# Gates, branches and mixer output: high and low input side by side on one load of the high weights, in blocks of 256 features

## The chip, the cores and the metric

The kernel runs on one core of one Trainium2 chip. Times are device microseconds of that core; several runs of a kernel are given as their median. The engines are TensorE (PE, with its weight loads shown as PEld), VectorE (DVE), ScalarE (ACT), GpSimd (POOL) and SyncE (SP), which here issues nearly all DMA transfers.

## The reference

One decoder layer over 256 tokens of 2048 features, in float32. The part that the change touches is the gated merge of the token mixer; the rest (a matrix-memory LSTM, a delta-rule recurrence, cross-attention into 256 memory tokens, a gated feed-forward layer with a short convolution) stays as it is.

```python
h = rms_norm(x, mix_pre_norm)
proj = h @ w_in                                  # 2048 -> 10536 columns
mlstm_p, rwkv_p, gate_p = split_cols(proj, ...)  # gate_p: 4096 columns
# ha: 256 x 1024, output of the mLSTM;  hb: 256 x 1024, output of RWKV-7
g_a, g_b = split_cols(gate_p, (D_MODEL, D_MODEL))
merged = sigmoid(g_a) * (ha @ w_branch_a) + sigmoid(g_b) * (hb @ w_branch_b)
y = merged @ w_out                               # 2048 -> 2048
x = x + rms_norm(y, mix_post_norm)
h = rms_norm(x, xattn_pre_norm);  m = rms_norm(mem, mem_norm)
x = x + rms_norm(cross_attention(h, m, ...), xattn_post_norm)
x = x + rms_norm(conv_glu_ffn(rms_norm(x, ffn_pre_norm), ...), ffn_post_norm)
```

## The kernel before

**Products in three matmuls.** Every float32 operand is split into a high part, rounded to the matmul's input type, and a low part, the rest. A product is then the sum of three: high weights with high input, high weights with low input, low weights with high input. An "fm" block gives features on partitions and the 256 tokens along the free axis; a "tm" block gives tokens on partitions and 512 features along the free axis. `block` (line 365) only notes what is to be done; `run` (line 435) goes through the list and issues everything.

**Narrow and wide fm blocks.** A narrow fm block has 512 output features: each 128 x 128 piece of weights (a step) takes three matmuls of 256 columns, which add up in one half of a PSUM bank; two features groups share a bank, a block has two banks. A wide block (line 475) has 256 output features. High and low input lie side by side in one tile, so that one matmul of 512 columns takes both on one load of the high weights: one half of the bank gets high times high, the other high times low. A second matmul of 256 columns adds low weights times high input to the first half. A wide block of two feature groups also has two banks. Who reads the result has to add the two halves. Before the change only the 58 blocks `w_fw` of the feed-forward layer are wide (line 1662), and `fw_evac` (line 1621) does that addition: two copies on ACT from PSUM, two additions on DVE.

**The way of a weight tile.** `Feed` (line 373) brings the weights in tiles of 512 KB (128 partitions x 1024 values): SP loads `raw` (three buffers), ACT rounds it to `wh` (line 402), DVE subtracts to `wl` (line 423; four buffers each). While tile i is multiplied, `run` issues the subtraction for tile i + 3 and the load for tile i + 6. A load waits until the subtraction three tiles earlier has freed its buffer. A 512-feature block has two k per tile, a block of 256 features four.

**Side work and its budget.** Everything but matmuls and weight casts is written as generators, cut in pieces by `yield`, and handed to `Spread` (line 73). `run` calls `half` once at the start of each weight tile and again between its k: a narrow tile of 512 features gives two calls, a wide one of 256 two as well, and a narrow tile of 256 features would give four. Each call adds 790 to a budget of DVE and 820 to one of ACT (estimated nanoseconds, at most 1200 saved up, at most 700 of debt kept), and then runs at most one piece of `bulk` (the evacuations, in their order) or `back`, if both budgets are positive, and those of `chains` whose turn has come, if neither is below -700. `need` issues all that is left of a task at once. At the start of each block `run` needs the evacuation of two blocks before. The engines then work in the order in which things were issued, each waiting for its operands.

**The order of blocks around the change.** After the projections of both mixers (two tm blocks for the output gate of the mLSTM come last, and `mlstm` runs on as part of the second one's evacuation, line 1140) come, for branch a and then branch b, gate blocks (2048 inputs, weights in `w_in`) ahead of branch blocks (1024 inputs): gate 0, gate 1, branch 0, gate 2, branch 1, gate 3, branch 2, branch 3 (line 1432). `gate_evac` (line 1232) multiplies by the row of inverse norms and applies the sigmoid; `br_evac` (line 1242) multiplies the branch by its gate, in branch b adds branch a, and splits the sum into `mgh` and `mgl`, the inputs of the mixer output. The recurrence (`rwkv`, a chain) runs beside them and ends in `hb_split`, which branch b needs (line 1399). Before branch b's last block `mem_prep` starts (line 1407): a chain with a piece every third call that loads the memory tokens in four transfers on SP, splits them and sums their squares; its sums over partitions are matmuls on PE (`st`, `stb`).

Then four mixer blocks (line 1455). `mo_xs` needs the last branch's evacuation when it comes to k = 12. Before the second mixer block `load_x` (line 1443) loads x again, 2 MB in two transfers on SP's queue. `y_evac` (line 1262) sums squares of the result and writes it, times a gain, to `z`; after the last block `column_of_sums` (line 344) folds the squares on DVE and sums them over partitions on PE. From that, `Residual` (line 1288) forms the new x and the input of the cross-attention's queries; meanwhile PE has the block `w_xk` to do, which needs only the memory tokens, and then `w_xq`, which needs the residual.

Of the kernel before, what the change touches and what calls it, by code (L numbers as in the profile page):

```python
# [15 lines left out]
P = 128  # L16
D = 2048
S = 256
# [134 lines left out]
def _layer(ctx, tc, nc, d, dbg):  # L153
# [119 lines left out]

    def bc(ap, n):
        return ap.unsqueeze(1).broadcast_to((ap.shape[0], n, ap.shape[1]))
# [97 lines left out]
    class Feed:  # L373
# [766 lines left out]
    def mlstm():  # L1140
# [38 lines left out]
        ha = [U(f"ha{i}", dt=F32R) for i in range(2)]  # L1179
        M["ha"] = ha  # L1180
        for k2 in range(4):
# [5 lines left out]
            for j in range(2):  # L1187
                k = k2 * 2 + j
                xsplit_gain(ha[0][:, k], ha[1][:, k], q[:, j], pcol("hn", k))
            yield  # L1190

    def hb_split():
# [6 lines left out]
        hb = [U(f"hb{i}", dt=F32R) for i in range(2)]  # L1199
        M["hb"] = hb  # L1200
# [8 lines left out]
        for p2 in range(4):  # L1209
# [18 lines left out]
            xsplit(hb[0][:, s2], hb[1][:, s2], M["bv"][:, s2])  # L1228
# [3 lines left out]
    def gate_evac(i, cb):  # L1232
        def gen(ps):
            sg = [T2("sg") for _ in range(2)]
            M["sg", i, cb] = sg
            for g in range(2):
                times(sg[g], ps[g], st0.rb)
                act.activation(sg[g], sg[g], AF.Sigmoid)
                yield
        return gen  # L1240

    def br_evac(i, cb):
        def gen(ps):
# [15 lines left out]
        return gen  # L1259


    def y_evac(b, st, key, gname):

        def gen(ps):
            if b == 0:
                M[key] = [U("z0"), U("z1")]
            z = M[key][b // 2]
# [5 lines left out]
            for g in range(2):  # L1273
                if not late:
                    st.add(ps[g])
                for j in range(2):
                    m = (b % 2) * 4 + g * 2 + j
                    act.activation(z[:, m], ps[g][:, j], AF.Copy, scale=pcol(gname, b * 4 + g * 2 + j))
                if g or not late:
                    yield  # L1280
            if b == 3 and not late:
# [591 lines left out]
```

## Time and profile before

| | us |
|---|---|
| median of 3 runs (1826.32 to 1827.95) | 1826.34 |
| the profiled execution | 1827.7 |
| its span | 1825.9 |
| PE busy, of the span | 1806.5 (99%) |
| DVE busy | 1349.3 (74%) |
| ACT busy | 1071.2 (59%) |
| mean granted TensorE clock | 0.997 |

The span runs from the first to the last instruction of the profiled execution; the time of that execution includes what lies around it. Rows of instruction views give start, duration (both in us from the span's start), engine, line, operation, output and inputs, shape and number; in brackets how long the engine was idle before, and for whom. Rows of windows give the stretch, its length, the busy time of PE, PEld, DVE, ACT and POOL (instructions in brackets), the granted clock, the DMA share and GB/s. Rows of the chain give start, length and what. Matmuls overlap in the pipe, so the duration in their rows is longer than the distance from one to the next. Line 66 is that of a helper through which all side work goes; there the tile names tell what it is: `sg` gates and branch sums, `mgh`/`mgl` the mixer's input, `mx`, `mem`, `stm` of `mem_prep`, `sty` and `z` of `y_evac`, `us`, `ul` of `fw_evac`.

### The profile page before, as it was taken

How to read it: one execution, taken by the hardware profiler on the slowest of the kernel's cores; microseconds unless marked ns; L12 is line 12 of the kernel's file. 1: busy time of each engine (PE TensorE's matmuls, PEld its weight loads, DVE VectorE, ACT ScalarE, POOL GpSimd, SP SyncE). 2: the span in 40 equal slices, each digit the busy share in tenths (PEclk: the TensorE clock that was granted, in tenths of full speed). 3: DMA queues.
4: the chain of work that ended last, by engine and by line, in shares of the span. 5: the costliest groups of instructions: out<-in, count | busy, mean ns of one | idle time of the engine just before them, and what ended most of it. 6: DMA issues, size and time to landing. Idle time of an engine off the chain costs nothing.

```text
span 1825.9 us, 32950 instructions
## 1 busy us (share of the span) xinstructions
PE 1806.5 (99%) x13182; PEld 1687.7 (92%) x13182; DVE 1349.3 (74%) x1954; ACT 1071.2 (59%) x1616; POOL 30.6 (2%) x53
## 2 busy tenths in 40 slices
PE   9999999999999999999999999999999999999998
PEld 8999988999999999899899999999999988888887
DVE  6879985666766766868887887877877876666665
ACT  6577355554544565666676767665656655555553
POOL 0100000000100000000000000000000000000000
PEclk9999999999999999999999999999999999999999
DMA  7655554354656675546566666666666666666664
GB/s 260 203 169 189 166 187 151 113 179 147 190 178 203 220 254 175 184 143 202 180 210 202 202 199 203 202 196 208 201 199 205 199 199 212 222 201 203 201 204 160
DMA packets 97899, 352.50 MB, mean 193 GB/s; under 512 B 11057, under 2 KB 11313, under 8 KB 97361
## 3 DMA queue, kind: packets, MB, share of 16 engines
q1 hardware_dynamic: 96496, 348.07, 59.8%
q8 instruction: 103, 1.69, 0.4%
q0 software_dynamic: 384, 1.18, 0.3%
q10 hardware_dynamic: 864, 1.15, 0.2%
q14 instruction: 52, 0.42, 0.1%
HBM read 347.73 MB, written 2.10 MB: 192 GB/s over the span
## 4 chain that ended last, share of the span: by engine, by line
PE 92%; DVE 4%; DMA 2%; issue 1%; ACT 1%; POOL 0%; DVEq 0%; POOLq 0%; ACTq 0%
PE fm L189 64%; PE tm L189 23%; DVE wl L423 1%; ACT wh L402 0%; DMA raw<-in_w_in_dram 0%; PE gram L189 0%; DMA raw<-in_w_mo_dram 0%; PE Y L189 0%; DVE ql L66 0%; DMA x<-in_x_dram 0%; PE lv L189 0%; DVE tg L66 0%; PE num L189 0%; DVE z L66 0%; PE X L189 0%
## 5 line engine op out<-in xcount | busy, mean ns | idle before, releaser
L423 DVE TENSOR_TENSOR wl<-raw,wh 128x1024 fp32r<-128x1024 f32 x640 | 780.2, 1222 | 319.5 <-ACT wh L402 316.1
L402 ACT CAST wh<-raw 128x1024 fp32r<-128x1024 f32 x640 | 669.4, 1048 | 372.6 <-PE fm L189 211.3
L189 PE MATMUL fm<-fx,wh 128*128 128x512 f32 (+1 forms) x2240 | 673.1, 364 | 0.6 <-ACT fx L66 0.6
L189 PE MATMUL fm<-fx,wl 128*128 128x256 f32 x2048 | 559.2, 273 | 1.5 <-DVE wl L423 1.3
L189 PEld LDWEIGHTS fm<-fx,wh 128*128 128x128 f32 x2240 | 409.1, 190 | 49.8 <-ACT fx L66 0.8
L189 PEld LDWEIGHTS fm<-fx,wl 128*128 128x128 f32 x2048 | 393.2, 192 | 3.2 <-DVE wl L423 3.2
L189 PE MATMUL fm<-hx,wh 128*128 128x256 f32 x2144 | 367.4, 278 | 1.2 <-ACT wh L413 1.2
L189 PEld LDWEIGHTS fm<-hx,wh 128*128 128x128 f32 x2144 | 327.0, 193 | 3.4 <-ACT hx L66 1.4
L189 PE MATMUL tm<-wh,as 128*128 128x512 f32 x1024 | 304.6, 379 | 0.0
L189 PE MATMUL fm<-hx,wl 128*128 128x256 f32 x1072 | 295.7, 276 | 0.5 <-DVE wl L423 0.4
L189 PEld LDWEIGHTS tm<-wh,as 128*128 128x128 f32 x1024 | 193.5, 189 | 27.5
L189 PEld LDWEIGHTS fm<-hx,wl 128*128 128x128 f32 x1072 | 206.5, 193 | 0.9 <-DVE wl L423 0.6
L189 PE MATMUL tm<-wl,as 128*128 128x512 f32 x512 | 194.0, 379 | 0.0
L189 PEld LDWEIGHTS tm<-wl,as 128*128 128x128 f32 x512 | 96.8, 189 | 13.7
L66 ACT CAST as<-ac 128x256 fp32r<-128x256 f32 x128 | 45.4, 402 | 104.0 <-PE tm L189 104.0
L66 DVE TENSOR_TENSOR as<-ac,as 128x256 fp32r<-128x256 f32 x128 | 48.5, 421 | 53.7 <-ACT as L66 53.7
L66 ACT COPY ul<-fm 128x256 f32<-128x256 f32 x116 | 40.6, 374 | 72.6 <-PE fm L189 72.6
L189 PE MATMUL tm<-wh,hx 128*128 128x512 f32 x256 | 77.2, 383 | 0.0
L189 PE MATMUL fm<-mgh,wl 128*128 128x256 f32 x256 | 70.5, 275 | 0.2 <-DVE wl L423 0.2
L189 PE MATMUL fm<-mgh,wh 128*128 128x256 f32 x256 | 70.6, 276 | 0.0
L189 PE MATMUL fm<-mgl,wh 128*128 128x256 f32 x256 | 70.4, 275 | 0.0
L66 DVE TENSOR_TENSOR us<-fm,ul 128x256 f32<-128x256 f32 x116 | 43.7, 419 | 26.3 <-ACT ul L66 26.3
(355 smaller groups left out, 1979.8 us busy)
## 6 DMA issues: line engine op xcount, KB each, us to landing
raw<-in_w_fw_dram SPq DMA_DIRECT2D x232, 512.0 KB, 4.0
raw<-in_w_in_dram SPq DMA_DIRECT2D x160, 512.0 KB, 3.5
raw<-in_w_fd_dram SPq DMA_DIRECT2D x128, 512.0 KB, 3.9
raw<-in_w_br_dram SPq DMA_DIRECT2D x32, 512.0 KB, 3.9
raw<-in_w_mo_dram SPq DMA_DIRECT2D x32, 512.0 KB, 3.8
raw<-in_w_fu_dram SPq DMA_DIRECT2D x24, 512.0 KB, 3.7
raw<-in_w_xk_dram SPq DMA_DIRECT2D x8, 512.0 KB, 3.5
raw<-in_w_xq_dram SPq DMA_DIRECT2D x8, 512.0 KB, 3.4
```

Source lines behind the costliest of these rows:

```text
L66: return f(out, *a, **k)
L189: pe.matmul(out, lhsT, rhs, start=start, stop=stop, skip_group_check=True)
L402: nc.scalar.copy(wh, r)
L423: nc.vector.tensor_sub(wl, r, self.st[self.nl][0])
```

## The change

The gate blocks, the branch blocks and the mixer blocks become blocks of 256 features: 16 gate blocks (their weights now in an array `w_g` of their own), 16 branch blocks, 8 mixer blocks. All are wide but the last four of branch b, which stay narrow, with three matmuls a step. The number of weight tiles and their size stay. `AHEAD` goes from 2 to 4, so that the same number of gate features is ahead of the branches; `mem_prep` now starts before the seventh block of branch b, `load_x` runs before the third mixer block.

`ha`, `hb` and `mg` are laid out so that high and low part of a k lie in one tile. The copies and additions of `fw_evac` move into a function `whole` with a tag of its own (two buffers), in which the sum is written over the copy; the gate, branch and mixer evacuations call it and then go on from SBUF. They handle one pair of features groups where they handled two. In branch b the evacuation has a second `yield`, after the product. The tiles for `wh` and `wl` lose 128 values of padding per partition, and so does `as` in the down projection, which also loses its offset of 112 values.

```diff
+    def whole(ps):
+
+        w = mp.tile([P, 2, S], F32, tag="lo", bufs=2, name="lo")
+        for i in range(2):
+            act.copy(w[:, i], ps[i][:, 1])
+        for i in range(2):
+            dve.tensor_add(w[:, i], ps[i][:, 0], w[:, i])
+        return w
...
-            w = wp.tile([P, 1024 + 128], F32R, tag=name, bufs=4, name=name)
+            w = wp.tile([P, 1024], F32R, tag=name, bufs=4, name=name)
...
-        ha = [U(f"ha{i}", dt=F32R) for i in range(2)]
-        M["ha"] = ha
+        M["ha"] = [U(f"ha{i}", [P, 2, 4, S], F32R) for i in range(2)]
...
     def gate_evac(i, cb):
         def gen(ps):
-            sg = [T2("sg") for _ in range(2)]
-            M["sg", i, cb] = sg
-            for g in range(2):
-                times(sg[g], ps[g], st0.rb)
-                act.activation(sg[g], sg[g], AF.Sigmoid)
-                yield
+            sg = M["sg", i, cb] = T2("sg")
+            times(sg, whole(ps), st0.rb)
+            act.activation(sg, sg, AF.Sigmoid)
+            yield
...
-                M["mg"] = [big("mgh", dt=F32R), big("mgl", dt=F32R)]
-            for g in range(2):
-                s2 = slice(cb * 4 + g * 2, cb * 4 + g * 2 + 2)
-                pa = M["pa"][cb // 2][:, (cb % 2) * 4 + g * 2:(cb % 2) * 4 + g * 2 + 2]
-                if i == 0:
-                    dve.tensor_mul(pa, ps[g], sg[g])
-                else:
-                    dve.tensor_mul(sg[g], ps[g], sg[g])
-                    dve.tensor_add(sg[g], sg[g], pa)
-                    xsplit(M["mg"][0][:, s2], M["mg"][1][:, s2], sg[g])
-                yield
+                M["mg"] = [big(f"mg{j}", [P, 2, 8, S], F32R) for j in range(2)]
+            s2 = slice(cb % 4 * 2, cb % 4 * 2 + 2)
+            pa = M["pa"][cb // 4][:, s2]
+            w = whole(ps) if len(ps) == 2 else ps[0]
+            if i == 0:
+                dve.tensor_mul(pa, w, sg)
+            else:
+                dve.tensor_mul(sg, w, sg)
+                yield
+                dve.tensor_add(sg, sg, pa)
+                mg = M["mg"][cb // 4]
+                xsplit(mg[:, 0, s2], mg[:, 1, s2], sg)
+            yield
...
-    def y_evac(b, st, key, gname):
+    def y_evac(b, st, key, gname, wide=False):
...
+            if wide:
+                ps = [whole(ps)]
...
     def gated(i, cb, before):
-        xs = lambda k: (M[("ha", "hb")[i]][0][:, k], M[("ha", "hb")[i]][1][:, k])
-        return block("fm", W("w_br", i * 4 + cb), xs, br_evac(i, cb), before=before)
-
-    AHEAD = 2
+        v = lambda k: M[("ha", "hb")[i]][k // 4][:, :, k % 4]
+        return block("fm", W("w_br", i * 8 + cb), lambda k: (v(k)[:, 0], v(k)[:, 1]), br_evac(i, cb), before=before,
+                     cols=256, wide=None if i and cb > 3 else v)
+
+    AHEAD = 4
     for i in range(2):
-        for cb in range(4 + AHEAD):
+        for cb in range(8 + AHEAD):
             if cb >= AHEAD:
                 before = None
                 if cb == AHEAD:
                     before = need_hb if i else lambda: side.need(o1["task"])
+                elif cb == 6 + AHEAD and i:
+                    before = start_mem
                 br = gated(i, cb - AHEAD, before)
-            if cb < 4:
-                block("fm", W("w_in", 12 + i * 4 + cb), xs0, gate_evac(i, cb))
-    br["before"] = start_mem
+            if cb < 8:
+                block("fm", W("w_g", i * 8 + cb), xs0, gate_evac(i, cb), cols=256, wide=lambda k: hx[:, :, k])
...
-    for b in range(4):
-        block("fm", W("w_mo", b), mo_xs, y_evac(b, sty, "z1", "postg"),
-              before=load_x if b == 1 else None)
+        return mgp(k)[:, 0], mgp(k)[:, 1]
+
+    for b in range(8):
+        block("fm", W("w_mo", b), mo_xs, y_evac(b, sty, "z1", "postg", True), before=load_x if b == 2 else None,
+              cols=256, wide=mgp)
...
-            us, lo = T2("us"), T2("ul")
-            for i in range(2):
-                act.copy(lo[:, i], ps[i][:, 1])
-            for i in range(2):
-                dve.tensor_add(us[:, i], ps[i][:, 0], lo[:, i])
+            us = whole(ps)
...
-            a = mp.tile([P, 1024 + 128], F32R, tag=f"au{n % 2}", bufs=1, name="as")[:, 112:112 + 1024]
+            a = mp.tile([P, 1024], F32R, tag=f"au{n % 2}", bufs=1, name="as")
```

More of the change, by code (lines that the diff above doesn't have):

```diff
@@ L1188, in mlstm @@
                 k = k2 * 2 + j
[L1189 removed]
+                ha = M["ha"][k // 4][:, :, k % 4]
+                xsplit_gain(ha[:, 0], ha[:, 1], q[:, j], pcol("hn", k))
             yield
@@ L1272, in gen @@
                 st.column()
[L1273 removed]
+            for g, v in enumerate(ps):
                 if not late:
[L1275 removed]
+                    st.add(v)
                 for j in range(2):
[L1277 to L1279 removed]
+                    m = b * len(ps) * 2 + g * 2 + j
+                    act.activation(z[m // 8][:, m % 8], v[:, j], AF.Copy, scale=pcol(gname, m))
+                if g == len(ps) - 1 or not late:
                     yield
[L1281 removed]
+            if b == (7 if wide else 3) and not late:
                 yield from st.column_of_sums()
```

17 lines of the change are left out of this document (9 added, 8 removed).

## The prediction

> **What bounds the kernel now.** I read the share of each engine, then the chain that ended last in order of time, then the stretches from the gates to the cross-attention by windows, and last the instructions of VectorE (DVE), ScalarE (ACT) and the DMA queue around the end of the branches, where the windows show the least room.
>
> ```profile
> PE 1806.5 (99%) x13182; PEld 1687.7 (92%) x13182; DVE 1349.3 (74%) x1954; ACT 1071.2 (59%) x1616; POOL 30.6 (2%) x53
> 512.45 128.65 PE fm L189 x1152
> 899.05 586.93 PE fm L189 x3583
> 1485.97 327.65 PE tm L189 x1518
> ```
>
> TensorE (PE) bounds it. The three rows of the chain are unbroken runs of matmuls, so a division gives what one costs: three of 256 columns are 3 x 128.65/1152 = 335.0 ns (second branch and first mixer block); a 512 and a 256 together 2 x 586.93/3583 = 327.6 ns (the wide blocks of the feed-forward layer); a 512 alone 327.65/1518 = 215.8 ns (down projection). 335.0/3 = 111.7, and 215.8 + 111.7 = 327.5: the rows agree, and two 256s on one load cost 2 x 111.7 - 215.8 = 7.6 ns more apart than as one 512.
>
> **The matmuls.** One step (a 128 x 128 piece of weights) goes from three matmuls to two, from 335.0 to 327.6 ns: 7.4 ns. Steps changed: gates 8 blocks x 16 k x 4 = 512; branches 8 x 8 x 4 = 256 less 4 x 8 x 2 = 64 left narrow = 192; mixer 4 x 16 x 4 = 256; together 960. 960 x 7.4 = **7.1 us** less. The bytes and the count of weight casts stay.
>
> The page "TensorE: Matmul & The Clock Gate" of the Trainium skill (section Back-to-back issue gap) gives a lone warm matmul N/2.4 + 2.5 ns, with the warning that a stream with weight loads behaves otherwise; by it two 256s cost only 2.5 ns more than one 512, and the gain would be 960 x 2.5 = 2.4 us. The 215.8 ns agrees with it; the 111.7 ns (109.2 by the formula) does not, and the sum goes by the rows.
>
> **The new evacuation.** `whole` adds two copies on ACT and two additions on DVE to each of 16 + 12 + 8 = 36 blocks (gates, branches, mixer). The feed-forward blocks do the same work:
>
> ```profile
> 1202.72 0.70 ACT L66 COPY ul<-fm 128x256 f32<-128x256 f32 x2 [1.34 <-PE fm L189]
> 1203.13 0.76 DVE L66 TENSOR_TENSOR us<-fm,ul 128x256 f32<-128x256 f32 x2 [0.49 <-ACT ul L66]
> 340.00:512.00 172.00, 172.00 (x1988) 169.06 (x1987) 117.00 (x170) 90.57 (x139) 8.88 (x8) 1.00 0.51 167
> 512.00:616.70 104.70, 104.70 (x940) 104.70 (x939) 65.86 (x67) 49.02 (x53) 0.00 (x0) 1.00 0.61 193
> 1000.00:1400.00 400.00, 400.00 (x2444) 367.78 (x2443) 318.22 (x463) 256.52 (x391) 0.00 (x0) 1.00 0.65 201
> ```
>
> 36 x 0.76 = 27 us of DVE and 36 x 0.70 = 25 us of ACT. Averaged over these windows (columns: length, busy PE, weight loads, DVE, ACT, POOL) that is hidden: DVE goes from 68% to some 77% in the first (20 of the blocks), from 63% to 69% in the second (8), and at 318/400 = 80% PE still runs without a gap in the third. If this cover is gone, a block costs up to 0.70 + 0.76 = 1.5 us. The new tag, the removed padding and the moved `as` tile change addresses, not counts: nothing, under the same cover (DVE could slow by a quarter there before it is full). The recurrence's last work, `hb`, has room too:
>
> ```profile
> L66 DVE TENSOR_TENSOR hb<-vT,hb x4: 692/742/743, 499.0 to 515.3; 128x512 fp32r<-128x512 f32 x4
> L189 PEld LDWEIGHTS fm<-hb,wh x256: 192/192/192, 530.9 to 616.5; 128*128 128x128 f32 x128
> ```
>
> It ends 15 us before its reader; nothing is taken for it.
>
> **Where the average hides a place: the last two branch blocks.** `half` hands out the side work. A narrow block of 256 features has four k per weight tile and so four calls of `half` in 2.68 us, where before there were two. `mem_prep` (a piece every third call) starts before branch block 6 at the same point of the matmul stream, but now 16 calls instead of 8 pass until the mixer, with the branch evacuations in the same stretch. Prices:
>
> ```profile
> 605.30:616.70 11.40, 11.40 (x105) 11.40 (x104) 9.20 (x11) 5.48 (x6) 0.00 (x0) 1.00 0.58 192
> 613.34 3.50 DVE L423 TENSOR_TENSOR wl<-raw,wh 128x1024 fp32r<-128x1024 f32 x3 [0.21 <-ACT wh L402]
> 616.75 0.68 DVE L66 TENSOR_TENSOR sg<-fm,sg 128x512 f32<-128x512 f32 x1
> 617.47 0.69 DVE L66 TENSOR_TENSOR sg<-sg,pa 128x512 f32<-128x512 f32 x1
> 619.02 0.76 DVE L66 TENSOR_TENSOR mgl<-sg,mgh 128x512 fp32r<-128x512 f32 x1 [0.86 <-ACT mgh L66]
> 625.64 2.36 DVE L423 TENSOR_TENSOR wl<-raw,wh 128x1024 fp32r<-128x1024 f32 x2 [0.72 <-ACT wh L402]
> 627.92 0.87 DVE L66 SCALAR_TENSOR_TENSOR mx<-mem,par,mx 128x256 fp32r<-128x256 f32 x2
> 628.71 0.68 DVE L66 TENSOR_TENSOR stm<-stm,sq 128x512 f32<-128x512 f32 x1
> 629.31 1.22 DVE L423 TENSOR_TENSOR wl<-raw,wh 128x1024 fp32r<-128x1024 f32 x1
> ```
>
> A weight subtraction (`wl`) takes DVE 3.50/3 = 1.17; a branch evacuation holds it 619.78 - 616.75 = 3.0, the wait for ACT's cast included; a piece of `mem_prep` 629.31 - 627.92 = 1.4 (the first 0.8, without the sum). The budget lets pieces 2 to 5 run before the mixer: it comes back at 790 per call, twice as often in time. DVE then owes, in the 10.7 us of blocks 6 and 7, 4 x 1.17 + 2 x 3.0 + 0.8 + 3 x 1.4 = 15.7 us: 5.0 too much. Blocks 4 and 5 are even (2 x 1.17 + 3.0 = 5.3 of 5.36 each), and so is the mixer's first block (4 x 1.17 + 3.0 + 2 x 1.4 = 10.5 of 10.5). The four 512 KB loads of `mem_prep` move with it in SP's queue, between the raw tiles; the third waits for pieces 2 and 3, but the raw tile behind it waits for a later `wl` of the same DVE anyway, and the DMA share of 0.58 leaves room: nothing more for them. What is late next is `wl`, made three tiles (8.0 us) ahead; with an evacuation in front of it, it is done some 4.5 us into its tile, a reserve of 3.5. So the first mixer tiles wait 5.0 - 3.5 = 1.5, and as the queue doesn't shrink until block 1, the last evacuation too: the new first mixer block needs feature tile k = 14 after 28 x 0.328 = 9.2 us, where the old one needed it after 56 x 0.335 = 18.8. That adds about 1.2. I take **2.7 us**; bounds 0 (the whole 8.0 holds) and 6 (5.0 of lag, and the last evacuation late by 1). For a wait speaks how near it was already: in the rows above, `wl` for the mixer's fifth tile ended at about 626.8, and that tile began at 616.7 + 4 x 2.68 = 627.4: 0.6 us to spare, at half the rate of pieces.
>
> **The x load**, 64 steps into the mixer in both kernels.
>
> ```profile
> 638.93 0.43 SPq L1414 DMA_DIRECT2D mem<-in_mem_dram  x1
> 641.46 0.90 SPq L1447 DMA_DIRECT2D xr<-in_x_dram  x2
> 654.90 0.38 PE L189 MATMUL fm<-mgh,wl 128*128 128x256 f32 x1 [0.19 <-DVE wl L423]
> 658.90 0.61 PE L189 MATMUL st<-ones,stm 128*128 128x1 f32 x4 [1.28 <-DVE stm L66]
> 638.00:648.80 10.80, 10.80 (x99) 10.80 (x98) 8.20 (x12) 10.77 (x19) 0.00 (x0) 1.00 0.88 346
> 648.80:659.50 10.70, 9.23 (x80) 8.85 (x80) 7.06 (x11) 5.44 (x8) 0.00 (x0) 1.00 0.63 229
> ```
>
> Weights queue behind 2 MB of x, and PE waits 0.19 + 1.28 us, the second time in order behind the sum of `mem_prep`. That sum is taken some 12 calls (16 us) earlier now: it moves off x, into the lag just told, and I leave its 1.28 in the sum. Against it, the tiles behind x come due at 2.62 us instead of 2.68, and each mixer block adds 1.5 us of copies and sums in ACT and DVE. **+0.9**; bounds -1.5 (both waits go) and +3 (ACT is 10.77 of 10.80 busy there, so two evacuations of 1.5 could show in full).
>
> **The mixer's end.** The sum of squares of z comes out one `half` earlier, but the new order on DVE is: two additions, square's sum, `wl`, fold.
>
> ```profile
> 705.48 0.83 ACT L66 ACTIVATE z<-fm,par 128x256 f32<-128x256 f32 x2
> 707.13 0.62 ACT L66 ACTIVATE sq<-fm 128x512 f32<-128x512 f32 x1
> 708.42 0.68 DVE L66 TENSOR_TENSOR sty<-sty,sq 128x512 f32<-128x512 f32 x1
> 709.14 0.42 DVE L66 TENSOR_TENSOR sty<-sty 128x256 f32<-128x256 f32 x1
> 709.48 1.22 DVE L423 TENSOR_TENSOR wl<-raw,wh 128x1024 fp32r<-128x1024 f32 x1
> 709.64 0.58 PE st L189 x4
> 720.00:740.00 20.00, 19.67 (x175) 19.33 (x174) 19.83 (x32) 13.60 (x22) 0.00 (x0) 1.00 0.49 156
> 740.00:760.00 20.00, 18.55 (x131) 17.24 (x132) 16.60 (x21) 13.05 (x17) 0.00 (x0) 1.00 0.66 211
> ```
>
> Before, the fold ran ahead of `wl`, and PE's column sums (`st`) came 709.64 - 705.35 = 4.3 us after the mixer's last matmul. Now: copies and additions 1.2, square 0.6, its sum 0.7; ACT meanwhile z 0.8 and cast 1.0, then `wl` 1.2 and fold 0.4: the sums come at 5.2. PE, in order, stands 2.5 us in front of them. What follows is set by DVE (19.83 of 20 us), in which PE idles 0.33 + 1.45 = 1.8 us anyway, so most of the 2.5 is absorbed; what counts is the residual's start, 5.2 - 4.3 = **+0.9** (bounds 0 and 2.5).
>
> **The mLSTM tail.** `run` forces the evacuation of two blocks ago. The first gate block now has 8 calls of `half`, not 16, for eleven pieces of `mlstm`; three transposes of `ha` are forced at once.
>
> ```profile
> 335.73 0.44 PE haT L1186 x4
> 336.71 0.88 DVE L66 SCALAR_TENSOR_TENSOR so<-num,rh,so 128x256 f32<-128x256 f32 x2
> ```
>
> The last waits for `so`, ready at 337.6, and would be reached near 337.1: **+0.5** (bounds 0 and 2, if ACT and DVE are late with casts behind them).
>
> **Sum** against the profiled execution (1827.7, span 1825.9): -7.1 + 2.7 + 0.9 + 0.9 + 0.5 = -2.1, so 1825.6 there; the median is 1826.34 and becomes **1824.2 us**.
>
> **Rivals.** (1) *The lag is hidden.* The reserve holds and x costs nothing new: -7.1 + 0.5 + 0.5 = -6.1, 1820.2. For: averages of 63% to 68% on DVE, a feed-forward at 80% without a gap. Against: the 0.6 us to spare. (2) *Slower: the ring of raw tiles.* A raw buffer comes free only when `wl` is made, so a late `wl` orders its successor late; behind x (7.6 us to land) cast 1.05 and `wl` 1.17, 9.8 us per three tiles of 7.9, lose 1.9 a turn. If the lag is still over the reserve of 3.5 us when x is ordered, it stays through two turns: 6.0 for the branches' end, 3 + 1.9 x 2 at x, 0.9 + 0.5: -7.1 + 14.2 = +7.1, 1833. For: ACT full in that window. Against: from mixer block 1 on, DVE owes 4 x 1.17 + 0.8 + 0.7 + 2.8 = 9.0 of 10.5 us, so 16 us after the overload the lag should be under it.
>
> ```profile
> L402 ACT CAST wh<-raw 128x1024 fp32r<-128x1024 f32 x640 | 669.4, 1048 | 372.6 <-PE fm L189 211.3
> xr<-in_x_dram SPq DMA_DIRECT2D x2, 1024.0 KB, 7.6
> ```
>
> (3) *The change gives less than it says*: a step saves only a third, 2.5 ns, because the 7.4 belongs to the order of loads in its own stage and not to the count of matmuls; 2.4 less and 5.0 back: 1828.9. Against: both rates are from one execution with PE full. The Trainium skill's formula, cited above, gives a saving of this size.
>
> **Chances.** Forecast 0.56 (own range 1821.5 to 1826.8), rival 1 0.26, rival 2 0.10, rival 3 0.04, something unseen 0.04. Range 1819.0 to 1829.0: rival 1 with all its gain at the low end, the upper bounds of the x load and the mixer's end together at the high one. This kernel's measurement tells about 0.2% (3.7 us) from no change: under 1822.7 lie rival 1 and a fifth of the forecast, 0.37; above 1830.0 rival 2 and half of the unseen, 0.12; the rest 0.51.
>
> **What would show it.** Steps: 512-column matmuls at `hx`, `ha`, `mg` and 327.6 ns a pair in unbroken runs. Lag: PE waits for `wl` and `mg` within 15 us of the mixer's start, none there before. Mixer's end: `st` waiting about 2.5 us for `sty`. Wrong: no wait at the mixer's start (rival 1), or waits that last beyond the x load (rival 2).

## The result, and the profile after

| | before | after |
|---|---|---|
| median of 6 runs, us | 1826.55 (1824.83 to 1827.95) | **1837.72** (1834.39 to 1840.59) |
| the profiled execution | 1827.7 | 1834.39 |
| its span | 1825.9 | 1832.6 |
| PE busy | 1806.5 | 1804.0 |

The ratio is **1.0061 [1.0048, 1.0074]**: slower, where 1824.2 was forecast and 1829.0 was the upper end of the range. The profiled execution of after is the fastest of its six; the other five ran at a mean granted clock of 0.995 to 0.997 where it had 0.998 (0.995 in the three runs of 1837.1, 1840.59 and 1840.01). So the trace accounts for 6.7 us of a loss of 11.2, and the clock, to which this text comes back, goes with the rest.

The chain of after (start, length, what) has the long run of the feed-forward layer again, to the hundredth:

```profile
905.54 586.93 PE fm L189 x3583
```

It began at 899.05 before, and all of the loss lies ahead of it. Where, is read from the rows of single tiles: behind the count come the shortest, median and longest instruction in ns, and the times of the first start and the last. First the kernel before, then after:

```profile
L189 PE MATMUL tm<-wl,hx x128: 378/379/379, 216.2 to 315.0; 128*128 128x512 f32 x128
L189 PE MATMUL fm<-ha,wh x256: 275/275/377, 376.7 to 484.0; 128*128 128x256 f32 x128
L189 PE MATMUL fm<-hb,wh x256: 275/275/275, 531.0 to 616.6; 128*128 128x256 f32 x128
L189 PE MATMUL fm<-mgh,wl x256: 275/275/377, 617.0 to 705.3; 128*128 128x256 f32 x128
```

```profile
L189 PE MATMUL tm<-wl,hx x128: 378/379/379, 214.1 to 312.9; 128*128 128x512 f32 x128
L189 PE MATMUL fm<-ha,wh x128: 382/382/483, 379.0 to 485.5; 128*128 128x512 f32 x128
L189 PE MATMUL fm<-hb,wh x192: 275/275/382, 534.0 to 618.1; 128*128 128x256 f32 x128, 128*128 128x512 f32 x64
L189 PE MATMUL fm<-mg,wl x256: 272/273/378, 618.5 to 707.9; 128*128 128x256 f32 x128
```

The starts give the stages. The steps are those of the prediction, at 7.4 ns each:

| stage, us | before | after | difference | by the steps | lost |
|---|---|---|---|---|---|
| up to the last o-gate matmul (ahead of the changed blocks) | 315.0 | 312.9 | -2.1 | 0 | - |
| to the first branch a matmul (128 steps) | 61.7 | 66.1 | +4.4 | -0.9 | **5.3** |
| to the first branch b matmul (384) | 154.3 | 155.0 | +0.7 | -2.8 | **3.5** |
| to the first mixer matmul with low weights (192) | 86.0 | 84.5 | -1.5 | -1.4 | 0 |
| mixer, from there to its last (256) | 88.3 | 89.4 | +1.1 | -1.9 | **3.0** |
| to the long run of the feed-forward layer | 193.7 | 197.6 | +3.9 | 0 | **3.9** |
| from there on | 926.9 | 927.1 | +0.2 | 0 | 0.2 |

The first row is not the work of the changed blocks: up to the first of these matmuls, in code in which the kernels differ only by the padding of `wh` and `wl`, the traces of this document lie between 214.1 and 217.5 us, and in the one of before the clock was halved for 3.4 us at 31.4 us. Counted from the last o-gate matmul, the change's trace is 8.8 us longer. The removed padding does not slow the work on weight tiles either: a cast takes 1047 ns by the median in both traces, a subtraction 1224 and 1225.

The row to the first mixer matmul is the cleanest: no wait in either kernel, 192 steps changed, 1.5 us less. The steps pay what was forecast; 15.7 us are lost in four places. The waits of PE name them (what waited, for whom, us in total, times, longest). Before, the stretches from 313 to 380, 380 to 536 and 705 to 718 us have no wait in this view, and that of the mixer has two:

```profile
PE st L189 <- DVE stm L66: 1.3, 1, 1.3
PE fm L189 <- DVE wl L423: 0.2, 1, 0.2
```

After, from 313 to 380 (the first three rows), from 380 to 536 (the next four) and from 610 to 725 us:

```profile
PE Tn L189 <- ACT au L66: 1.3, 1, 1.3
PE Tn L189 <- DVE au L66: 1.1, 1, 1.1
PE U L189 <- DVE ha L66: 1.0, 2, 0.7
...
PE fm L189 <- DVE wl L432: 0.7, 1, 0.7
PE X L189 <- ACT m L66: 0.7, 1, 0.7
PE zg L189 <- DVE gwl L66: 0.4, 1, 0.4
PE zg L189 <- DVE gwh L66: 0.4, 1, 0.4
...
PE st L189 <- DVE sty L66: 2.9, 1, 2.9
PE st L189 <- DVE stm L66: 1.2, 1, 1.2
PE fm L189 <- DVE wl L432: 1.2, 2, 0.8
PE fm L189 <- DVE mg L66: 0.8, 1, 0.8
PE stb L189 <- POOL sty_c L236: 0.5, 1, 0.5
```

This view counts a wait from the modelled end of the matmul ahead of it and leaves short ones out, so its rows add up to less than a stage lost: 2.2 us of 3.5 from branch a to branch b.

**The burst behind the mLSTM** is the largest. These are rows of the timeline of after, PE's without its block matmuls, then ACT's, then DVE's:

```profile
335.02 1.47 PE L1194 MATMUL haT<-con,so 128*128 128x128 f32 x12
339.46 0.68 PE L189 MATMUL U<-au,mt 64*64 64x64 f32 x16 [0.74 <-DVE ha L66]
345.56 0.33 PE L189 MATMUL Tn<-au,bg 128*64 128x64 f32 x2 [1.29 <-ACT au L66]
347.01 0.62 PE L189 MATMUL Tn<-au,bg 128*64 128x64 f32 x13 [1.12 <-DVE au L66]
...
343.68 0.63 ACT L66 ACTIVATE sg<-sg 128x512 f32<-128x512 f32 x1 [1.50 <-DVE sg L66]
344.21 1.03 ACT L411 CAST wh<-raw 128x1024 fp32r<-128x1024 f32 x1
345.14 0.63 ACT L66 COPY au<-U 64x256 f32<-64x256 f32 x2
...
342.07 0.75 DVE L66 TENSOR_TENSOR lo<-fm,lo 128x256 f32<-128x256 f32 x2
342.85 0.79 DVE L66 TENSOR_TENSOR sg<-lo,st_b 128x512 f32<-128x512 f32 x1
345.27 1.23 DVE L432 TENSOR_TENSOR wl<-raw,wh 128x1024 fp32r<-128x1024 f32 x1 [1.63 <-ACT wh L411]
346.53 0.77 DVE L66 COPY au<-U 64x256 f32<-64x256 f32 x2
```

Twelve transposes come at once, because the second gate block needs all of `mlstm`; ACT and DVE then hand `ha` to and fro until 342 (`U` waits meanwhile), go on with the first gate block's copies, additions, product and sigmoid, then with a cast and its subtraction, and only then copy `U` to `au`. The recurrence's `Tn` stands in PE's order and waits for that copy. The clock then falls, as windows of 3.4 us show (length, busy PE, PEld, DVE, ACT, POOL, granted clock, DMA share, GB/s):

```profile
344.20:347.60 3.40, 0.98 (x22) 0.78 (x23) 2.27 (x4) 2.52 (x5) 0.00 (x0) 0.99 0.05 13
347.60:351.00 3.40, 3.40 (x62) 3.17 (x60) 1.80 (x3) 0.73 (x2) 0.00 (x0) 0.50 0.83 276
```

**The mixer's end**, the second place, in the timeline of after (DVE, then PE without block matmuls):

```profile
708.99 0.75 DVE L66 TENSOR_TENSOR lo<-fm,lo 128x256 f32<-128x256 f32 x2
710.44 0.69 DVE L66 TENSOR_TENSOR sty<-sty,sq 128x512 f32<-128x512 f32 x1 [0.70 <-ACT sq L66]
712.17 1.22 DVE L432 TENSOR_TENSOR wl<-raw,wh 128x1024 fp32r<-128x1024 f32 x1 [1.04 <-ACT wh L411]
713.31 0.42 DVE L66 TENSOR_TENSOR sty<-sty 128x256 f32<-128x256 f32 x1
...
713.78 0.61 PE L189 MATMUL st<-ones,sty 128*128 128x1 f32 x4 [2.89 <-DVE sty L66]
716.34 0.71 PE L189 MATMUL stb<-con,sty_c 128*128 128x128 f32 x4 [0.50 <-POOL sty_c L236]
```

The order on DVE is the one forecast: additions, square's sum, `wl`, fold. The column sums come 713.78 - 707.95 = 5.8 us after the mixer's last matmul, where 5.2 were forecast and 4.3 was the time before.

### The profile page after: what moved, and what is told of

Read it like the earlier page. It is cut to its first block, busy times and chain, and to the rows that moved or that the text cites. A ratio compares the mean times of both kernels' runs of the same rounds, so it can differ in the third digit from the quotient of the medians.

```text
span 1832.6 us, 31158 instructions
## 1 busy us (share of the span) xinstructions
PE 1804.0 (98%) x12222; PEld 1656.2 (90%) x12222; DVE 1375.9 (75%) x2026; ACT 1090.7 (60%) x1688; POOL 32.5 (2%) x53
## 4 chain that ended last, share of the span: by engine, by line
PE 83%; DVE 8%; ACT 3%; DMA 3%; issue 2%; POOL 0%; DVEq 0%; SPq 0%; ACTq 0%; POOLq 0%
PE fm L189 56%; PE tm L189 23%; DVE wl L432 4%; ACT wh L411 2%; DMA raw<-in_w_mo_dram 1%; DVE lo L66 1%; PE Y L189 0%; DMA raw<-in_w_xv_dram 0%; DMA raw<-in_w_g_dram 0%; PE gram L189 0%; DVE z L66 0%; DVE ql L66 0%; ACT z L66 0%; DVE tg L66 0%; DVE sg L66 0%
## 5 line engine op out<-in xcount | busy, mean ns | idle before, releaser
L411 ACT CAST wh<-raw 128x1024 fp32r<-128x1024 f32 x640 | 667.2, 1047 | 332.3 <-PE fm L189 154.7
L189 PE MATMUL fm<-hx,wh 128*128 128x256 f32 (+1 forms) x1632 | 363.3, 312 | 1.0 <-ACT wh L422 1.0
L189 PEld LDWEIGHTS fm<-hx,wh 128*128 128x128 f32 x1632 | 268.0, 192 | 16.1 <-ACT hx L66 1.3
L66 ACT COPY lo<-fm 128x256 f32<-128x256 f32 x188 | 64.4, 372 | 84.9 <-PE fm L189 84.4
L189 PEld LDWEIGHTS tm<-wl,as 128*128 128x128 f32 x512 | 96.8, 189 | 13.7
L66 DVE TENSOR_TENSOR lo<-fm,lo 128x256 f32<-128x256 f32 x188 | 70.9, 419 | 28.2 <-ACT lo L66 28.1
L189 PE MATMUL fm<-mg,wh 128*128 128x512 f32 x256 | 84.7, 383 | 0.8 <-DVE mg L66 0.8
L189 PE MATMUL fm<-mg,wl 128*128 128x256 f32 x256 | 70.2, 274 | 1.3 <-DVE wl L432 1.2
L66 DVE SCALAR_TENSOR_TENSOR tg<-lo,cv,tg 128x255 f32<-128x255 f32 x116 | 55.8, 481 | 2.1
```

The costliest lines, as they stand in the source:

```text
L66: return f(out, *a, **k)
L189: pe.matmul(out, lhsT, rhs, start=start, stop=stop, skip_group_check=True)
L411: nc.scalar.copy(wh, r)
```

## The experiments

All are compared with runs of the kernel before on the same chip (medians 1825.9 to 1826.2). Medians are of 4 to 11 runs.

| kernel | median, us | ratio to before |
|---|---|---|
| the change | 1837.72 | 1.0061 [1.0048, 1.0074] |
| e1: mLSTM tail apart | 1831.51 | 1.0029 [1.0018, 1.0039] |
| e2: fold ahead of `wl` | 1833.97 | 1.0042 [1.0027, 1.0057] |
| e3: two calls a tile | 1837.34 | 1.0060 [1.0038, 1.0082] |
| e4: e1 + e2 + e3 | 1830.11 | 1.0020 [1.0011, 1.0029] |
| e5: e1 + all evacuations cut | 1842.33 | 1.0090 [1.0076, 1.0103] |
| e6: e1 + memory tokens earlier | 1832.95 | 1.0034 [1.0021, 1.0046] |
| e7: e1 + last mixer block narrow | 1829.96 | 1.0020 [1.0011, 1.0030] |
| e8: e5 + e6 + e7 | 1841.05 | 1.0083 [1.0069, 1.0097] |
| e9: e1 + e3, cut where there is room, mixer narrow | **1818.89** | **0.9962 [0.9949, 0.9976]** |
| e10: the change, mixer narrow | 1829.09 | 1.0018 [1.0009, 1.0027] |
| e11: e9, evacuations uncut | 1822.25 | 0.9977 [0.9968, 0.9986] |
| e12: e9, mixer wide but its last block | 1827.39 | 1.0006 [0.9997, 1.0015] |

### One place at a time

**e1, the mLSTM tail as a task of its own**, needed by the first branch block and no longer by the second gate block:

```diff
             if n == 1:
-                yield from mlstm()
+                tasks["ml"] = side.add(mlstm())
...
-                    before = need_hb if i else lambda: side.need(o1["task"])
+                    before = need_hb if i else lambda: side.need(tasks["ml"])
```

> Edit: the mLSTM tail becomes a task of its own, needed by the first branch block, so that the forced evacuation at the start of the second gate block no longer issues three transposes of ha and their splits at once. Theory A (that burst is the largest loss: the recurrence's matmuls U and Tn stand behind it, 2.6 and 2.8 us of PE waiting at 338 to 347 us, and the granted clock falls to half for 3.4 us after it): these waits and the half-clock stretch go, the granted clock of the runs returns to 0.997 or more, and the time falls 5 to 9 us below the changed kernel, to 1829 to 1833. Rival B (the added copies and sums of 36 blocks load DVE and ACT everywhere, no single place counts): PE's waits between 313 and 520 us only move, the time falls by less than 2 us.

The median is 6.2 us below the change, the span 5.9 (1826.7). In its trace PE waits for nothing from 313 to 380 us, and the clock stays up in the ten microseconds in question and behind them:

```profile
337.00:347.00 10.00, 10.00 (x107) 8.95 (x107) 7.18 (x12) 6.45 (x14) 0.00 (x0) 1.00 0.30 107
```

In the change PE is busy 6.62 of these 10.00 us. So the burst goes when the tail is spread, and the clock's fall behind it goes with it; what is left, 5.6 us over the kernel before, is elsewhere.

**e2, the mixer's last fold ahead of the next weight subtraction** on DVE; PE's order is the same:

```diff
-                if g == len(ps) - 1 or not late:
+                if (g == len(ps) - 1 or not late) and not (wide and b == 7):
                     yield
...
-                yield from st.column_of_sums()
+                yield from st.column_of_sums(2 if wide else 1)
```

> Edit: after the last mixer block the fold of the squares is issued with the evacuation, ahead of the weight subtraction; the column sums stay at the same place in PE's order. One DVE instruction changes places with its neighbour. Theory A (PE stands in front of the column sums because the fold is behind a weight subtraction): the wait of 3.05 us before st at 713.8 falls to 1.5 or less, and the time falls by 1 to 2.5 us. Rival B (what follows is set by DVE's 35 us of residual work, so where PE waits doesn't matter): the wait goes but the first feed-forward matmul comes within 0.5 us of where it came, time the same within 0.5 us.

The wait for `sty` falls from 2.89 to 0.67 us, but the next one grows:

```profile
711.39 0.61 PE L189 MATMUL st<-ones,sty 128*128 128x1 f32 x4 [0.67 <-DVE sty L66]
714.95 0.71 PE L189 MATMUL stb<-con,sty_c 128*128 128x128 f32 x4 [1.51 <-POOL sty_c L236]
```

The column sums come 2.4 us earlier, the broadcast `stb` behind them 1.4, and the span is 1.8 us shorter. The median is 3.75 lower, with runs that overlap (1832.58 to 1837.27, the change 1834.39 to 1840.59); the part beyond 1.8 can't be told from the clock (0.997 in all four runs, 0.995 to 0.998 in those of the change).

**e3, two pieces of side work per tile in the last four blocks of branch b**, as before the change:

```diff
-                    if kj + 1 < s.shape[1] and (not b["wide"] or kj % 2):
+                    if kj + 1 < s.shape[1] and (s.shape[1] == 2 or kj % 2):
```

> Edit: a narrow block of 256 features calls the side work twice per weight tile as all others do, not four times. Theory A (the doubled calls pack mem_prep and the evacuations into the last two branch blocks): the waits of 2.3 us for mg and wl in the first 15 us of the mixer go; mem_prep's sum comes some 10 us later, near x again, and may cost what it did before (1.4 us); time 1 to 3 us lower. Rival B (the waits come from the evacuation's own length, not from the calls): waits of 1.5 us or more stay at the mixer's start, time the same within 1 us.

The waits at the mixer's start are gone, and nothing is won, since the memory tokens' sums now come behind the x load. In the mixer stage this is its one wait, and the clock halves behind it:

```profile
PE st L189 <- DVE stm L66: 4.9, 1, 4.9
```

**e4, the three together:**

> All three edits together. Theory A (the steps pay their 7.1 us and the three places are what eats them): 1820 to 1824 us, 0.1% to 0.4% faster than the kernel before. Rival B (the load of the added evacuation work is the cause): slower than the kernel before, above 1828 us.

1830.11, only 1.4 below e1, which is within the spread of the runs, and slower than the kernel before. The first theory (three places, each with a small repair) falls: PE still waited 1.4 us for `wl`, 1.2 for `lv`, 0.5 for `X` and 0.4 for `zg`, e2's part had left one of 1.5 for `stb`, and e3's part had brought one of 4.1 for `stm`.

### Order or amount

The trace of e1 showed where more was lost: the recurrence's matmuls (`X`, `zg`) and weight tiles between branch a and branch b, behind evacuations in which ACT copies, DVE adds and ACT again takes the sigmoid, each engine standing for the other. **e5** cuts these pieces:

```diff
         for i in range(2):
             act.copy(w[:, i], ps[i][:, 1])
+        yield
         for i in range(2):
             dve.tensor_add(w[:, i], ps[i][:, 0], w[:, i])
...
-            times(sg, whole(ps), st0.rb)
+            w = yield from whole_in_two(ps)
+            times(sg, w, st0.rb)
+            yield
             act.activation(sg, sg, AF.Sigmoid)
```

> The run with the mLSTM tail as a task of its own (median 1831.5, span 1826.7, waits of PE between the first branch a and the first branch b matmul 4.8 us), and in it the gate and branch evacuations cut: one piece for ACT's two copies, one for DVE's two additions and the product, one for the sigmoid or the branch sum. The work is the same. Theory A2 (the waits come from engines standing in order: DVE in front of ACT's copies, ACT in front of the sigmoid's operand, weight casts and the recurrence's steps queued behind): those waits fall from 4.8 to under 2, the median by 2 to 4, to 1827.5 to 1829.5. Rival B (the amount of added work, 0.76 us of DVE and 0.70 of ACT a block, delays what is behind it however it is cut): waits stay over 4, median within 1 of 1831.5.

Neither. From the first branch a to the first branch b matmul (373.4 to 526.3) it took 152.9 us instead of 156.1, and by the view of waits 1.2 us were left of 2.1 (the 4.8 of the expectation counts every start later than nominal, the short ones too); so the order theory holds there. But behind branch b's start PE then stood for banks of PSUM:

```profile
534.47 0.45 PE L189 MATMUL fm<-hx,wh 128*128 128x512 f32 x1 [2.70 <-DVE lo L66]
```

A wide branch block has four calls; with three pieces in place of one the evacuations fell behind, and the lag went on into the mixer: 5.2 us at `sty`, and 10.8 us of median lost against e1. In this trace the clock was halved at 535.0, 627.2 and 719.4 us, for 13.7 us together; by an estimate of half of that, up to 6.8 us of the loss are the clock's.

**e6, memory tokens two blocks earlier**, with e3's two calls a tile, so that as many pieces run before the mixer in twice the time:

```diff
-                elif cb == 6 + AHEAD and i:
+                elif cb == 4 + AHEAD and i:
```

> The run with the mLSTM tail as a task of its own, and in it the last four blocks of branch b hand out two pieces per weight tile instead of four, and the preparation of the memory tokens starts two blocks earlier (before branch block 4 instead of 6), so that as many pieces as in the changed kernel run before the mixer, over twice the time. Theory A2 (the lag at the mixer's start is the doubled rate of pieces; moved into time that is free, it costs nothing): the waits for mg and wl at the mixer's start, 2.0 us, go to under 0.3, the wait of the memory sums stays at 1.4 or under, median 1828.5 to 1830. Rival C (the last evacuations of branch b and the mixer's own make the lag, whatever the memory tokens do): at least 1.2 us of the waits stay, median 1831 to 1832. Rival D (as when the calls alone were halved: the memory sums then come behind the x load and PE stands 4 to 5 us there): 1832 to 1835.

Rival C in what the trace shows: the waits for `mg` and `wl` (0.8 us each) at the mixer's start and that of 1.2 for `stm` are where they were. The median, 1832.95, lies within the spread of e1's runs (1828.53 to 1837.27). So the rate of pieces alone does not make the lag. What goes with it in DVE's rows is how many pieces of `mem_prep` stand between the third last write of `mg` and the last one: four in the change, three in e6, one in e3 and in e12 below. The last write ends 10.5, 10.4, 6.3 and 6.0 us after the mixer's first matmul, and PE waits for it in the first two alone. e3 and e6 have the same calls in these blocks and differ there only in where `mem_prep` starts.

**e7, the mixer's last block narrow**, without copies and additions in front of the sums:

```diff
-              cols=256, wide=mgp)
+              cols=256, wide=mgp if b < 7 else None)
```

> The run with the mLSTM tail as a task of its own, and in it the mixer's last block alone is narrow, so that no copies and additions stand between its last matmul and the sum of squares; it loses 32 of the 960 steps, 0.24 us. Theory A2: the column sums come 4.0 to 4.8 us after the last mixer matmul instead of 5.6, PE waits under 2 us there instead of 2.8 + 0.7, and the residual starts that much earlier: median 1828.5 to 1830. Rival (the residual and the squares after it are set by DVE over the next 20 us, so the start hardly matters): within 0.8 of 1831.5.

In the rows it is as the theory had it: `st` waits 1.6 us instead of 2.6 and comes 711.98 - 707.4 = 4.6 us after the last matmul; `stb` still waits 0.5. The median is 1.55 lower, with runs that overlap (1827.62 to 1832.24, e1 1828.53 to 1837.27), so it does not show the gain by itself. And behind the x load, from 658 to 663 us, this trace waits 2.0 us for weight tiles where that of e1 waits 0.5, though the blocks up to there are the same: waits of this size come and go from one execution to the next.

**e8, e5 to e7 together:**

> All four: the mLSTM tail as a task of its own, cut evacuations, memory tokens two blocks earlier at half the rate of pieces, mixer's last block narrow. Theory A2 (the change pays its 7 us in full once the waits that it makes are closed): 1831.5 less 2 to 4, less 2, less 2 to 2.5, so 1822 to 1825.5, below the kernel before (1826). Rival B (the added work costs what the steps save, wherever it is put): 1828 or more.

1841.05, within 1.3 of e5: the cut's new lag hides the rest. It settles nothing on the amount of work.

### Parts apart

**e9** keeps the cut where the side work has calls to spare, and leaves the mixer output as it was:

```diff
+            cut = i == 0 or cb < 3
+            w = yield from whole_in_two(ps, cut)
...
-    for b in range(8):
-        block("fm", W("w_mo", b), mo_xs, y_evac(b, sty, "z1", "postg", True), before=load_x if b == 2 else None,
-              cols=256, wide=mgp)
+    for b in range(4):
+        block("fm", W("w_mo", b), mo_xs, y_evac(b, sty, "z1", "postg"), before=load_x if b == 1 else None)
```

> Gates and branches wide, the mixer output in its four narrow blocks of before; the mLSTM tail as a task of its own; the evacuations of both gates and branches cut in pieces only where the side work has calls to spare (all of branch a, the first three gate blocks of branch b); two pieces of side work per weight tile in the last four branch blocks. 704 of the 960 steps are left, 5.2 us. Theory A2 (work in order, place by place): from the first gate matmul to the first branch b matmul as with all evacuations cut, 212.5 us, no wait for banks after it, 84.3 more to the mixer, so 296.8 instead of 301.6 in the kernel before; mixer and what follows as before: median 1820.5 to 1823. Rival B (the added copies and additions cost what the steps save): 1825.5 or more. Between them, 1823 to 1825.5, some of the waits have come back at other places.

**1818.89**, below the expected range and 7.15 us below the kernel before, with every copy and addition of the gates and branches still in it. Its rows answer to those of the two kernels above:

```profile
L189 PE MATMUL tm<-wl,hx x128: 378/379/379, 214.5 to 313.3; 128*128 128x512 f32 x128
L189 PE MATMUL fm<-ha,wh x128: 382/382/483, 373.1 to 480.0; 128*128 128x512 f32 x128
L189 PE MATMUL fm<-hb,wh x192: 275/275/382, 526.1 to 610.2; 128*128 128x256 f32 x128, 128*128 128x512 f32 x64
L189 PE MATMUL fm<-mg,wl x256: 275/275/275, 610.6 to 697.0; 128*128 128x256 f32 x128
```

From the o-gate to branch b 212.8 us (216.0 before), to the mixer 84.5 (86.0), mixer 86.4 (88.3). From 313 to 725 us one wait of 1.2 us is left. Rival B falls: the amount of evacuation work is hidden once it is issued in pieces that fit. By stages, gates and branches are 4.7 us shorter, where the 704 steps make 5.2. The mixer is 1.9 shorter though its blocks are those of before: it has no wait now where it had 1.3 + 0.2, and why those went wasn't tried. The kernel before was not run with the mLSTM tail apart, so how much of the 7.15 us needs the wide blocks is not shown.

**e10, the change with the mixer alone put back** (the second part of the diff of e9):

> The changed kernel with one part undone: the mixer output in its four narrow blocks of before, gates and branches as changed. It gives up 256 steps, 1.9 us, and the mixer's own losses go (waits at its start 2.3, at its end 3.9 - 0.8 of that in the order of the fold). Theory A2 (the parts' losses add up): 1837.7 + 1.9 - 2.3 - 3.9 = 1833.4, with the burst of the mLSTM tail and its half clock still in it; range 1832 to 1835. Rival (the mixer's part is a gain, and its waits are only passed on from the branches): 1838 or more.

1829.09, better than the range: putting the mixer back wins 8.6 us by medians and 5.0 by spans (1827.6), against 4.3 expected. The sign and the places are right. The clock of the timed runs (0.996 to 0.998 here, 0.995 to 0.998 in the change) goes with the difference between 5.0 and 8.6.

**e11, e9 with every evacuation in one piece:**

> The run with gates and branches wide, the mixer narrow and the mLSTM tail apart (median 1818.9), with one part undone: every gate and branch evacuation is one piece again, as in the change. The work is the same. Theory A2 (the order within a piece costs the waits of the recurrence and of the weight tiles): from the first branch a to the first branch b matmul 156.1 us instead of 153.0, median 1821 to 1823.5. Rival (the cut only moves waits, as it did in the run where all evacuations were cut): within 1 of 1818.9.

1822.25. The same work in another order costs 3.4 us by medians, and its span is 2.6 us longer, 1.9 of them where they were expected, from branch a to branch b (373.3 to 528.2, 154.9 us instead of 153.0, with 156.1 expected). The waits from 380 to 536 us:

```profile
PE X L189 <- ACT m L66: 0.5, 1, 0.5
PE fm L189 <- DVE wl L432: 0.4, 1, 0.4
PE zg L189 <- DVE gwh L66: 0.4, 1, 0.4
```

They come to 1.3 us, and e9 has its one wait of 1.2 (for `lo`) in the same stretch. So the 1.9 us are seen from start to start; in this view they hardly show, as most of PE's late starts are too short for it.

**e12, e9 with the mixer wide but for its last block:**

> The same run (1818.9) with the other part done again: seven of the eight mixer blocks wide, the last one narrow. 224 steps, 1.7 us, are won. Theory A2 (the mixer stage has no room for the copies and additions beside the memory tokens, the x load and the sums of squares): PE waits in the stage and at its end come to 6 to 9 us instead of none, median 1823 to 1827. Rival (the mixer's losses in the change were passed on from lag that the branches left; with that gone it gains): 1817 to 1818.5.

1827.39: 8.5 us over e9, 0.4 beyond the expected range, although 224 steps, 1.7 us, are saved. So the mixer's losses are its own, not passed on from the branches. The row of the wait, ACT's ahead of it, and windows of 3.4 us around it:

```profile
648.73 1.01 PE L189 MATMUL st<-ones,stm 128*128 128x1 f32 x4 [3.92 <-DVE stm L66]
...
646.04 1.04 ACT L422 CAST wh<-raw 128x1024 fp32r<-128x1024 f32 x1 [3.35 <-DMA raw<-in_w_mo_dram]
```

```profile
644.30:647.70 3.40, 0.51 (x4) 0.21 (x2) 0.73 (x2) 1.59 (x3) 0.00 (x0) 1.00 0.82 287
647.70:651.10 3.40, 2.37 (x9) 2.19 (x10) 2.33 (x5) 1.73 (x4) 0.00 (x0) 0.50 0.68 242
```

The windows end at a half clock that lasts 6.8 us. A weight tile lands late behind x, its cast and subtraction are late, the fold of `stm` stands behind the subtraction on DVE, and PE, in order, behind the fold. It begins as the prediction's second rival does, with a late tile behind x, but what PE waits for is the fold. The narrow mixer of e9 has the late tile too (ACT waits 4.33 us for it and casts at 645.70); there the fold of `stm` ran at 642.82, ahead of that tile's subtraction, while in e12 it comes behind it, at 648.26. Why it comes a tile later in e12 stays open.

## Why the prediction was wrong

It failed on the sign, and by 13.5 us. By its own steps, with the losses of the stage table:

- **The matmuls, -7.1: right.** 192 steps without a wait took 1.5 us less (1.42 by the sum). Rival 3, with 2.5 ns a step, would have given 0.5. One reading is wrong: two matmuls of 256 columns do not share a load. The row of loads for `hb` in the prediction counts 256, as many as the matmuls in the rows of the result; over the whole span the change has 960 fewer of both (13182 before, 12222 after). So the 7.4 ns are the price of a matmul together with its load.
- **The evacuation, hidden: wrong as it was argued.** The averages (DVE 68%, 63%) do show that the work fits, and e9 shows that it can be hidden. But an average says nothing of what stands behind a piece in an engine's order. Hidden behind block matmuls it costs little (0.5 us in the gate and branch stages of e9, 4.7 won where the steps make 5.2); in front of an operand of the recurrence or of a weight tile it costs the time for which it holds the engine, the other engine's included (e11: 3.4 us by medians for the same work in another order).
- **`hb`, "nothing is taken": wrong, 3.5 us.** The step looked at the end of the recurrence, 15 us ahead of its reader. The recurrence's own matmuls stand in PE's order all the way; each waits for what ACT or DVE has in front of its operand (`X` 0.7, `zg` 0.4 + 0.4), and a weight tile does too (`wl` 0.7). These listed waits come to 2.2 of the 3.5.
- **The mLSTM tail, +0.5 with bounds 0 and 2: the worst miss, 5.3 us.** The step saw that `run` forces it and that three transposes come at once, and priced only their wait for `so`. The splits of `ha` behind them, the first gate block's evacuation with its four new instructions, and the recurrence's `U` and `Tn` behind those were not counted, nor the clock, which is some 1.4 of the 5.3 (by e3, see the last section). e1 spread the tail and came out 6.2 us lower by medians; its stage up to branch a takes 60.2 us instead of 66.1.
- **The last two branch blocks, +2.7: right in size, not in its cause.** With the x load (+0.9) 3.6 were forecast for the stage, and 3.0 lost. The waits for `wl` and `mg` stood where they were said to. But e6, at half the rate of calls, kept them, so the doubled rate is not the cause; what goes with them is how many pieces of `mem_prep` stand among the last evacuations. Nor did pieces 2 to 5 run ahead of the mixer: on DVE one did, at 614.09 us, and three came in the mixer's first 6 us. That the size agrees is luck in part.
- **The mixer's end, +0.9 with bounds 0 and 2.5: mis-sized, 3.9.** Column sums at 5.8 us (5.2 forecast) and a wait of 2.9 (2.5 forecast) were nearly right. "Most of the 2.5 is absorbed" was wrong: the cross-attention's wait for `qT` fell only from 1.5 to 0.4, and `wl` waits in the same 60 us rose from 0.3 to 1.4, which gave it back. DVE is busy 19.83 of 20.00 us from 723 to 743, and the copies and additions that made PE wait had delayed DVE as well; that this is why nothing was absorbed is a reading, not a run.
- **The range.** It reached only as far as places with a bound had one. Two places were costed at nothing with no upper end, and no term stood for a fall of the granted clock.

The rival on the slower side (1833) was nearest in time, but its place, the ring of raw tiles behind x, is not where the change lost: there the stage lost what was forecast, and the wait for `wl` behind x is 0.4 us. Longer waits behind x showed in e6 and e7 (2.0 us for weight tiles) and, with the fold of `stm`, in e3, e4 and e12 (3.9 to 4.9).

## What to carry to other kernels

Where PE works in order and is the bound, price an edit to side work by what stands behind it: list each matmul that PE will reach in the next 10 us, and for each the work that ACT and DVE have in front of its operand. Pieces that go from ACT to DVE and back should be cut where the engine would stand, but only as far as there are calls to issue the pieces before their banks are needed. Judge a change part by part: here gates and branches gain 0.4% together with the repairs (the repairs alone were not run), and the mixer output, the same edit, loses more than that.

## What the runs showed of the hardware

**The granted clock falls without a long idle time.** After windows of 3.4 us in which PE was busy 0.98 us (the change) and 0.51 us (e12), the next 3.4 and 6.8 us were granted half the clock. In the change's window two waits, of 1.29 and 1.12 us, make up the idle time. No busy time is a clean border: half a clock followed 1.65 us in before (window from 27.95 us) and 1.76 in e6 (from 709.30), while the change kept the full clock at the mixer's end, where its wait of 2.89 us lay across two windows with 1.50 and 2.05 us busy (from 709.4).

**The same waits can meet a window or miss it.** e3 has the burst too, with the same waits of 1.29 us (until 348.99) and 1.12 us (until 350.44). But on a grid of 3.41 us counted back from its half clock at 656.62 us a border falls between the two, at 349.39, and the clock stays up:

```profile
345.98:349.39 3.41, 2.04 (x13) 1.50 (x11) 1.75 (x3) 2.29 (x5) 0.00 (x0) 1.00 0.01 2
349.39:352.80 3.41, 2.36 (x68) 2.23 (x70) 3.05 (x6) 1.30 (x3) 0.00 (x0) 1.00 0.42 154
```

Its stage from the o-gate to branch a takes 64.7 us, where the change, e2 and e10, with the half clock, take 66.0 to 66.2. So this window at half clock cost 1.3 to 1.5 us; an estimate of half of 3.4 gives 1.7.

The Trainium skill ("TensorE: Matmul & The Clock Gate", section What's actually happening) says that the clock is halved by default and after an idle window of about 3.4 us, and that the window runs freely. The length and the dependence on where a wait falls agree with these rows; but no window here was idle throughout, PE was busy 0.98 of 3.4 us in the change's. Its advice to leave no idle gap over about 3 us (section Why this matters for your kernels) is too mild for this kernel: two waits of 1.29 and 1.12 us were enough.

**Waits and the spread of the runs.** Over its runs the mean clock is 0.995 in e3 and e5 (longest waits 4.9 and 5.2 us) and 0.9986 in e9 (1.2 us from 313 to 725 us), though 0.997 in e8 (4.2 us); and the six runs of the change lie 6.2 us apart, at 0.998 in the fastest and 0.995 in the slowest. Whether the same wait meets a window would explain that, but in the runs without a trace it is not shown. Nor is the clock all of it: e1's fastest and slowest runs (1828.53 and 1837.27) both had 0.997.
